# More filler products on TensorE ahead of the first modulation rows

## The chip, the cores and the metric

The kernel runs on one core of a Trainium2 chip. The core has five engines that work side by side, each on its own queue of instructions, in order: TensorE (PE in the profile, matrix products; PEld is its loading of the stationary operand), VectorE (DVE), ScalarE (ACT), GpSimd (POOL) and SyncE (SP), which here issues the transfers. The metric is the device time of one execution in microseconds; lower is better.

## The reference

One layer of a trunk with two parallel groups of heads. 1024 latent tokens and 128 context tokens, each of 1024 channels, are normalised, scaled and shifted by a modulation that comes from a conditioning vector, and multiplied with one input weight; a gated position mixer and a latent attention follow, and an output projection is added to the residual under a gate.

```python
def _front(x, cond, norm_g, w_ada, b_ada, w_in, ...):
    mod = jax.nn.silu(cond) @ w_ada + b_ada
    shift, scale, gate = jnp.split(mod[:, None, :], 3, axis=-1)
    h = _rmsnorm(x, norm_g) * (1 + scale) + shift
    u, v, g_a, c_q, c_kv, k_rope, g_b = _split_in(h @ w_in)
...
def _back(x, gate, a_out, attn, g_b, w_o):
    y = jnp.concatenate([a_out, attn * jax.nn.silu(g_b)], axis=-1) @ w_o
    return x + gate * y
```

All inputs are float32: `w_ada` is 1024 x 3072, `w_in` 1024 x 2496. What matters for the change is the first line: no column of `h` can be made before the shift and scale of its 128 channels are there, and these are a product of the conditioning vector with a slice of `w_ada`.

## The kernel before

The 1152 tokens are nine tiles of 128 (eight latent, one context), the 1024 channels eight slices k of 128. The first stage makes, slice by slice, the modulation, the transposed and modulated tokens `h` (split into a high and a low part, so that three products of them give the accuracy of float32), and the v projection of the tokens, accumulated in PSUM over the slices (`vacc`).

For slice k the stage does the following.

- `load_k(k)` (L376) has SyncE load the slice of `w_ada` in two halves of 512 KB (`load_ada`, L318, one transfer each, L322; each half holds four of the eight blocks of the contraction) and the v weights (`load_wv`, L282).
- `mod_rows(k)` (L330) makes the modulation rows: for each half i four products, one for each strip j of 32 columns of the array, into four strips of the PSUM tile `modp`. Each product of float32 is two instructions in the trace, so a half is eight.
- `mod_copy(k)` (L338): VectorE copies the rows to SBUF (`rows`).
- `mod_cols(k)` (L342): two products with `sel` add the four strips and turn the rows into columns, again in `modp`.
- `mod_act(k)` (L346): ScalarE adds the bias and the norm's gain and writes the columns `at`.
- `h_pe(k, g)` (L432): TensorE transposes three token tiles into `xT`; `h_ev(k, g)` (L436): ScalarE and VectorE modulate them with `at` and split them into the high and low part (`area`).
- `v_block` and `v_block_late` (L439, L443) add the slice to `vacc`.

Ahead of slice 0, token tiles 0 to 2 are loaded, their squares are summed and they are scaled by the root of their mean (ScalarE, VectorE and GpSimd). Behind the first group's modulation the same is done with tiles 3 to 5, in the queues of ScalarE and VectorE.

TensorE, ScalarE, VectorE and GpSimd run this stage in the order in which the lines are written (`manual_schedule`, L455), and so does SyncE; no planner moves anything here. `keep_warm(n)` (L458) writes n products of the identity with a matrix of ones into a PSUM tile `warm` that nothing reads: filler products. They wait for no other engine but for the identity at the start. Before the change there are 24 at the start (L462), and 6, 4, 3 and 2 between the products of slices 0 and 1 (L494 to L506). In TensorE's queue the start is: 24 fillers, `mod_rows(0)`, `mod_cols(0)`, three transposes, 6 fillers, the first products of `vacc`.

Of the kernel before, what the change touches and what calls it, by code (L numbers as in the profile page):

```python
# [81 lines left out]
def f32(ap):  # L82
    return ap.bitcast(F32)
# [3 lines left out]
def tile_hymba_step(ctx: ExitStack, tc: tile.TileContext, I, O):  # L87
# [198 lines left out]
    def load_x(t, i):  # L286
        xt[t] = slot(i, f"x{t}", [1024])
        nc.sync.dma_start(xt[t], I["x"][t])

    def load_x_aside(t):  # L290

        c0 = 2 * P * t - 9 * P
        xt[t] = mixA[:, :, c0 : c0 + 256]
        nc.sync.dma_start(xt[t], I["x"][t].rearrange("p (h c) -> p h c", h=4))
# [6 lines left out]
    def split_w1(k, raw, n, pre):  # L301
        h_ = w1.tile([P, n], F32R, tag=f"wh{k}", name=f"{pre}h{k}")
        l_ = w1.tile([P, n], F32R, tag=f"wl{k}", name=f"{pre}l{k}")
        pool_copy(h_, raw)
        G.tensor_tensor(l_, raw, f32(h_), op=ALU.subtract)
        return h_, l_
# [20 lines left out]

    modp = psa.tile([P, 512], F32, tag="acc", name="modp")

    def mod_rows(k):  # L330


        for i in range(2):
            for j in range(4):
                kk = 4 * i + j
                T.matmul(modp[32 * j : 32 * j + 32, 0:256], csp[:, kk, :], ada[k][kk], start=i == 0, stop=i == 1)

    def mod_copy(k):  # L338
        rowsb[k] = va.tile([P, 256], F32, tag="acc", name=f"rows{k}", bufs=2)
        V.tensor_copy(rowsb[k], modp[:, 0:256])  # L340

    def mod_cols(k):  # L342
        for c in range(2):
            T.matmul(modp[:, 256 + 2 * c : 258 + 2 * c], rowsb[k][:, c * P : (c + 1) * P], sel, start=True, stop=True)

    def mod_act(k):  # L346
        S.activation(at[:, k, :, 0], modp[:, 256:258], AF.Identity, bias=badaT[:, k, 0:1])
        S.activation(at[:, k, :, 1], modp[:, 258:260], AF.Identity, bias=gbias[:, k : k + 1], scale=normg[:, k : k + 1])
# [27 lines left out]
    def load_k(k):  # L376
        if k < NK:
            ada[k] = load_ada(k, ADA[k % 3])
            load_wv(k)
# [7 lines left out]
    def load_w2(i):  # L387
        w2raw[i] = slot(4 + i % 2, f"w2r{i}", [8, P])
        nc.sync.dma_start(w2raw[i], I["w_t"][i])
# [11 lines left out]
    def square(eng, t, out):  # L401
        junk = vb.tile([P, 1024], BF16, tag="junk" if eng is S else "junkV", name=f"junk{t}")
        if len(xt[t].shape) == 3:
            junk = junk.rearrange("p (h c) -> p h c", h=4)
        if eng is S:
            S.activation(junk, xt[t], AF.Square, accum_out=out)
        else:
            V.scalar_tensor_tensor(junk, xt[t], 1.0, xt[t], op0=ALU.mult, op1=ALU.mult, accum_out=out)

    def scale_x(eng, t, r):  # L410
        if eng is S:
            S.activation(xt[t], xt[t], AF.Copy, scale=r)
        elif eng is G:
            G.tensor_scalar(xt[t], xt[t], r, 0.0, op0=ALU.mult, op1=ALU.add)
        else:
            V.tensor_scalar(xt[t], xt[t], r, None, op0=ALU.mult)

    def row_roots(ssq):

        root = vb.tile([P, 3], F32, tag="xroot", name="xroot", bufs=2)  # L420
        v = vb.tile([P, 3], F32, tag="x3v", name="x3v", bufs=2)
        r = vb.tile([P, 3], F32, tag="x3r", name="x3r", bufs=2)
        u = vb.tile([P, 3], F32, tag="x3t", name="x3t", bufs=2)
        S.activation(root, ssq, AF.Sqrt, bias=epsb, scale=1.0 / 1024.0)
        V.tensor_scalar(v, ssq, 1.0 / 1024.0, EPS, op0=ALU.mult, op1=ALU.add)
        V.reciprocal(r, root)
        V.tensor_tensor(u, r, r, op=ALU.mult)
        V.scalar_tensor_tensor(u, u, -0.5, v, op0=ALU.mult, op1=ALU.mult)
        V.scalar_tensor_tensor(r, u, 1.5, r, op0=ALU.add, op1=ALU.mult)
        return r  # L430

    def h_pe(k, g):  # L432
        xps[k, g] = pst.tile([P, 512], F32, tag="t", name=f"xT{k}{g}")
        transposes(k, [3 * g, 3 * g + 1, 3 * g + 2], xps[k, g])

    def h_ev(k, g):  # L436
        modulate(k, g, xps[k, g][:, :GW])

    def v_block(k, ts_):  # L439
        for t in ts_:  # L440
            v_terms(k, t, vacc[t])

    def v_block_late(k, ts_):  # L443

        for t in ts_:
            g, j = t // 3, t % 3
            a = hh[k, g][:, j * P : (j + 1) * P]
            T.matmul(vacc[t], a, wvh[k], start=k == 0, stop=False)
            T.matmul(vacc[t], a, wvl[k], start=False, stop=False)
        for t in ts_:  # L450
            g, j = t // 3, t % 3
            T.matmul(vacc[t], hl[k, g][:, j * P : (j + 1) * P], wvh[k], start=False, stop=False)

    engines = {mybir.EngineType.PE, mybir.EngineType.Activation, mybir.EngineType.DVE, mybir.EngineType.Pool}
    with tc.manual_schedule(engines=engines):  # L455
        warm = psa.tile([P, 512], F32, tag="acc", name="warm")

        def keep_warm(n):  # L458
            for _ in range(n):
                T.matmul(warm[:, 0:P], ident, ones, start=True, stop=True)  # L460

        keep_warm(24)  # L462
        for t in (0, 1, 2):
            load_x(t, 6 + t)
        load_k(0)
        for t in (3, 4, 5):
            load_x(t, 6 + t)
        load_k(1)
        load_k(2)
        for t in range(5):  # L470
            vacc[t] = psa.tile([P, 512], F32, tag="acc", name=f"vacc{t}")
        ssq = [vb.tile([P, 3], F32, tag="ssq", name=f"ssq{i}", bufs=2) for i in range(2)]
        for j, eng in enumerate((S, V, S)):
            square(eng, j, ssq[0][:, j : j + 1])
        r0 = row_roots(ssq[0])
        for j, eng in enumerate((S, V, G)):
            scale_x(eng, j, r0[:, j : j + 1])
        wvh[0] = w1.tile([P, 512], F32R, tag="wh0", name="vh0")
        wvl[0] = w1.tile([P, 512], F32R, tag="wl0", name="vl0")
        S.copy(wvh[0], wvr[0])  # L480
        mod_rows(0)
        mod_copy(0)
        mod_cols(0)
        mod_act(0)
        G.tensor_tensor(wvl[0], wvr[0], f32(wvh[0]), op=ALU.subtract)
        h_pe(0, 0)
        h_ev(0, 0)
        for j, eng in enumerate((S, S, V)):
            square(eng, 3 + j, ssq[1][:, j : j + 1])
        r1 = row_roots(ssq[1])  # L490
        for j, eng in enumerate((S, V, V)):
            scale_x(eng, 3 + j, r1[:, j : j + 1])
        wvh[1], wvl[1] = split_w1(1, wvr[1], 512, "v")
        keep_warm(6)  # L494
        v_block_late(0, (0, 1, 2))
        keep_warm(4)
        mod_rows(1)
        mod_copy(1)
        keep_warm(3)
        h_pe(0, 1)  # L500
        mod_cols(1)
        h_pe(1, 0)
        h_ev(0, 1)
        mod_act(1)
        h_ev(1, 0)
        keep_warm(2)  # L506
        v_block_late(0, (3, 4))
        load_k(3)
        h_pe(1, 1)
        mod_rows(2)  # L510
        h_ev(1, 1)
        mod_copy(2)
        wvh[2], wvl[2] = split_w1(2, wvr[2], 512, "v")
        v_block_late(1, (0, 1))
        for k in range(2, NK):

            more = k + 1 < NK
            load_k(k + 2)
            mod_cols(k)
            h_pe(k, 0)  # L520
            h_pe(k, 1)
            mod_act(k)
            h_ev(k, 0)
            h_ev(k, 1)
            if more:
                wvh[k + 1], wvl[k + 1] = split_w1(k + 1, wvr[k + 1], 512, "v")
                mod_rows(k + 1)
                mod_copy(k + 1)
            v_block(k - 1, (0, 1, 2, 3, 4) if k > 2 else (2, 3, 4))
            if k == 2:  # L530
                for t in (6, 7, 8):
                    load_x_aside(t)
            if k == 4:
                load_w2(0)
                load_w2(1)
                nc.sync.dma_start(wsT, I["wsT"])
                nc.sync.dma_start(bsb, I["b_s"].broadcast_to([P, 512]))
                nc.sync.dma_start(kvg, I["kv_g"].broadcast_to([P, P]))
                ssq2 = vb.tile([P, 3], F32, tag="ssq", name="ssq6", bufs=2)
                for j, eng in enumerate((S, V, V)):  # L540
                    square(eng, 6 + j, ssq2[:, j : j + 1])
            if k == 5:
                r2 = row_roots(ssq2)
                for j, eng in enumerate((G, G, V)):
                    scale_x(eng, 6 + j, r2[:, j : j + 1])
# [217 lines left out]
    for i in range(3, 12):  # L763
# [10 lines left out]
        if i >= 4:  # L774
            k = i - 4
# [832 lines left out]
```

## Time and profile before

| | before |
|---|---|
| median of three runs | 635.0 us (634.12 to 635.34) |
| the profiled execution | 633.38 us |
| its span, first to last instruction | 631.6 us |
| mean granted clock of TensorE | 0.995 |
| TensorE busy | 614.2 us, 97% of the span |
| VectorE busy | 366.5 us, 58% |
| ScalarE busy | 259.4 us, 41% |
| GpSimd busy | 181.8 us, 29% |

The profile shows one execution. Busy is the time that an engine's instructions cover; a matrix product is pipelined, so its row is longer than the distance to the next one, and the pace is read from the starts. "PEclk" is the clock that the throttle granted to TensorE, 1.00 being full. The rest of the text counts time in us from the start of the span.

### The profile page before, as it was taken

The numbers are of one execution on the slowest core, as the hardware profiler recorded it, in microseconds if no ns is written. First come the engines' busy times: TensorE is split into PE (matmuls) and PEld (weight loads), VectorE is DVE, ScalarE is ACT, GpSimd is POOL, SyncE is SP. The second block draws the span as 40 slices with busy tenths as digits, with TensorE's granted clock in tenths as the row PEclk, the third lists the DMA queues.
The fourth block names the chain that finished last, engine by engine and source line by source line (L and its number), as shares of the span: only waits on it lengthen the run. The fifth ranks groups of instructions, "written<-read, shape, count | busy, mean of one in ns | idle before, by whom it ended". The sixth has DMA issues, their size and how long they took to land.

```text
span 631.6 us, 9907 instructions
## 1 busy us (share of the span) xinstructions
PE 614.2 (97%) x3733; PEld 557.1 (88%) x3733; DVE 366.5 (58%) x907; ACT 259.4 (41%) x615; POOL 181.8 (29%) x217
## 2 busy tenths in 40 slices
PE   7999999999999999999979999999999999999995
PEld 6677889999999999999967999999999988888884
DVE  3666447048556200667866665776766755487655
ACT  8456753112111111455646556555555543132212
POOL 2545123247532510433443221332222341000001
PEclk9999999999999999999989999999999999999999
DMA  8993100042322320000010000000101012524311
GB/s 324 353 356 107 34 0 2 1 141 109 113 92 72 110 88 13 25 2 1 2 39 1 2 2 0 1 1 35 34 1 34 33 68 87 181 100 134 104 64 66
DMA packets 17120, 46.32 MB, mean 73 GB/s; under 512 B 1953, under 2 KB 6449, under 8 KB 17073
## 3 DMA queue, kind: packets, MB, share of 16 engines
q1 hardware_dynamic: 16928, 45.51, 21.1%
q8 instruction: 29, 0.48, 0.3%
q10 hardware_dynamic: 144, 0.20, 0.1%
q14 instruction: 19, 0.15, 0.1%
HBM read 40.87 MB, written 4.83 MB: 72 GB/s over the span
## 4 chain that ended last, share of the span: by engine, by line
PE 91%; DVE 4%; ACT 2%; DMA 1%; issue 1%; SPq 0%; ACTq 0%
PE tp L670 6%; PE tp L150 6%; PE tp L152 6%; PE tp L151 6%; PE pT L1134 5%; PE w L1383 5%; PE w L1382 5%; PE w L1381 5%; PE s L1087 3%; PE o L1158 3%; PE o L1160 3%; PE s L1088 3%; PE s L1089 3%; PE s L1090 3%; PE o L1159 3%; PE s L1091 3%
## 5 line engine op out<-in xcount | busy, mean ns | idle before, releaser
L104 DVE TENSOR_TENSOR pl<-pT,ph 128x512 fp32r<-128x512 f32 x81 | 55.5, 687 | 48.0 <-ACT ph L1138 47.8
L1078 POOL TENSOR_SCALAR e<-e,rs 128x1280 f32<-128x1280 f32 x32 | 43.0, 1343 | 134.1 <-DVE rs L1077 116.3
L152 PE MATMUL tp<-area,w2l 128*128 128x384 f32 x216 | 72.5, 336 | 0.0
L150 PE MATMUL tp<-area,w2h 128*128 128x384 f32 x216 | 72.5, 336 | 0.0
L151 PE MATMUL tp<-area,w2h 128*128 128x384 f32 x216 | 72.5, 336 | 0.0
L1072 ACT ACTIVATE e<-s,nb,scl 128x256 f32<-128x256 f32 x64 | 56.1, 881 | 37.6 <-DVE nb L1066 37.6
L1138 ACT CAST ph<-pT 128x512 fp32r<-128x512 f32 x80 | 45.4, 589 | 43.5 <-PE pT L1134 40.6
L1134 PE MATMUL pT<-ident,e 128*128 128x128 f32 x320 | 47.8, 272 | 0.7 <-DVE pl L104 0.7
L1158 PE MATMUL o<-ph,vh 128*128 128x256 f32 x160 | 47.8, 299 | 0.0
L104 DVE TENSOR_TENSOR w2l<-w2r,w2h 128x1024 fp32r<-128x1024 f32 x12 | 20.2, 1685 | 46.1 <-POOL w2h L107 46.1
L1160 PE MATMUL o<-ph,vl 128*128 128x256 f32 x160 | 44.9, 281 | 0.0
L1159 PE MATMUL o<-pl,vh 128*128 128x256 f32 x160 | 44.7, 280 | 0.0
L1383 PE MATMUL w<-area,ml 128*128 128x512 f32 (+1 forms) x114 | 43.2, 379 | 0.0
L1134 PEld LDWEIGHTS pT<-ident,e 128*128 128x128 f32 x320 | 37.5, 140 | 4.4 <-DVE pl L104 1.5
L1062 DVE TENSOR_REDUCE m<-s 128x1 f32<-128x1024 f32 x32 | 38.9, 1216 | 4.0 <-PE s L1091 4.0
L150 PEld LDWEIGHTS tp<-area,w2h 128*128 128x128 f32 x216 | 40.5, 188 | 0.6 <-issue 0.5
L151 PEld LDWEIGHTS tp<-area,w2h 128*128 128x128 f32 x216 | 40.5, 188 | 0.2
L152 PEld LDWEIGHTS tp<-area,w2l 128*128 128x128 f32 x216 | 40.5, 188 | 0.0
L1087 PE MATMUL s<-kch,area 128*128 128x512 f32 (+2 forms) x100 | 39.5, 395 | 0.6 <-DVE area L104 0.6
L670 PE MATMUL tp<-area,w2h 128*128 128x384 f32 x144 | 37.4, 340 | 0.0
L1089 PE MATMUL s<-kch,area 128*128 128x512 f32 (+2 forms) x100 | 35.8, 358 | 0.0
L1088 PE MATMUL s<-kcl,area 128*128 128x512 f32 (+2 forms) x100 | 35.7, 357 | 0.0
(309 smaller groups left out, 1590.0 us busy)
## 6 DMA issues: line engine op xcount, KB each, us to landing
ada<-in_ada_ss SPq DMA_DIRECT2D x16, 512.0 KB, 10.9
w2r<-in_w_t SPq DMA_DIRECT2D x12, 512.0 KB, 4.3
xr<-in_x SPq DMA_DIRECT2D x9, 512.0 KB, 5.1
adag<-in_ada_g SPq DMA_DIRECT2D x8, 512.0 KB
wor<-in_w_o SPq DMA_DIRECT2D x8, 512.0 KB, 3.4
out_y<-y SPq DMA_DIRECT2D x8, 512.0 KB, 2.7
x<-in_x SPq DMA_DIRECT2D x6, 512.0 KB, 8.7
wvr<-in_w_v SPq DMA_DIRECT2D x8, 256.0 KB, 8.6
```

The costliest lines, as they stand in the source:

```text
L104: V.tensor_tensor(lo, src, f32(hi), op=ALU.subtract)
L150: T.matmul(ps, wh, xh, start=j == 0, stop=False)
L151: T.matmul(ps, wh, xl, start=False, stop=False)
L152: T.matmul(ps, wl, xh, start=False, stop=j == n - 1)
L670: T.matmul(tps[i, g][:, :GW], w_[i][:, k, :], x_[k, g], start=k == 0 and j == 0, stop=k == NK - 1 and j == 2)
L1072: S.activation(e[:, sl], src, AF.Exp, bias=nb, scale=scl[:, t : t + 1], accum_out=su[:, i : i + 1])
L1087: T.matmul(ps, qh_, kch[:, sl], start=True, stop=False)
L1134: T.transpose(ps[:, w : w + P], es[t, h][:, c * P : (c + 1) * P], ident)
L1158: T.matmul(o, vh[:, kt, :], ph[:, sl], start=c == 0, stop=False)
L1159: T.matmul(o, vh[:, kt, :], pl[:, sl], start=False, stop=False)
L1160: T.matmul(o, vl[:, kt, :], ph[:, sl], start=False, stop=c == n - 1)
L1383: T.matmul(ps, b, woh[k][:, c0:c1], start=False, stop=k == NK - 1)
```

## The change

Three calls are changed, all in TensorE's queue ahead of the first modulation columns. The fillers at the start are 32 in place of 24. `mod_rows` gets a parameter: with `between=4`, which slice 0 alone uses, four fillers stand between the products of the first and of the second half (`keep_warm(0)` ahead of the first half does nothing). Four more fillers stand between the call that copies the rows, `mod_copy(0)`, and `mod_cols(0)`; the copy is VectorE's, so in TensorE's queue they follow the second half's products. Together 16 fillers are added. No transfer, no copy and no other engine's instruction is added or removed.

```diff
-    def mod_rows(k):
+    def mod_rows(k, between=0):
         for i in range(2):
+            keep_warm(i * between)
             for j in range(4):
                 kk = 4 * i + j
                 T.matmul(modp[32 * j : 32 * j + 32, 0:256], csp[:, kk, :], ada[k][kk], start=i == 0, stop=i == 1)
...
-        keep_warm(24)
+        keep_warm(32)
...
-        mod_rows(0)
+        mod_rows(0, 4)
         mod_copy(0)
+        keep_warm(4)
         mod_cols(0)
         mod_act(0)
```

## The prediction

> **What bounds the kernel now.** I read the page's busy table and its chain first, then the stretch in which the change lies, instruction by instruction.
>
> ```profile
> span 631.6 us, 9907 instructions
> PE 614.2 (97%) x3733; PEld 557.1 (88%) x3733; DVE 366.5 (58%) x907; ACT 259.4 (41%) x615; POOL 181.8 (29%) x217
> ...
> PE 91%; DVE 4%; ACT 2%; DMA 1%; issue 1%; SPq 0%; ACTq 0%
> ```
>
> TensorE is the bound: 97% of the span is covered, and 91% of the chain that ended last is its own work. What matters is therefore not whether TensorE has idle time somewhere, but whether a product added to its queue finds idle time just where it is put. The next view is its timeline over the stretch from the first filler product (L460) to the second layer of modulation rows.
>
> ```profile
> 1.36 7.06 PE L460 MATMUL warm<-ones,ident 128*128 128x128 f32 x48 [1.36 <-POOL ident masks.py:199]
> 9.62 0.64 PE L336 MATMUL modp<-ada,csp 128*32 128x256 f32 x8 [1.20 <-DMA ada<-in_ada_ss]
> 10.80 0.64 PE L336 MATMUL modp<-ada,csp 128*32 128x256 f32 x8 [0.54 <-DMA ada<-in_ada_ss]
> 11.99 0.61 PE L344 MATMUL modp<-sel,rows 128*128 128x2 f32 x4 [0.55 <-DVE rows L340]
> 12.46 0.52 PE L352 MATMUL xT<-ident,x 128*128 128x128 f32 x3
> 12.82 1.50 PE L460 MATMUL warm<-ones,ident 128*128 128x128 f32 x12
> ...
> 16.25 1.05 PE L460 MATMUL warm<-ones,ident 128*128 128x128 f32 x8
> 17.23 1.29 PE L336 MATMUL modp<-ada,csp 128*32 128x256 f32 x16
> 18.45 0.94 PE L460 MATMUL warm<-ones,ident 128*128 128x128 f32 x6
> 19.22 0.49 PE L352 MATMUL xT<-ident,x 128*128 128x128 f32 x3
> ```
>
> Each row is start, length, engine, line, operation and, in brackets, the idle time ahead of it with its cause. The three holes that the change fills stand there: 1.20 us until the first half of the weights has landed, 0.54 us until the second half has, and 0.55 us while VectorE copies the rows. The 24 filler products are 48 instructions, so one call of the loop body is two.
>
> The chain of this stretch in order of time says what comes late now:
>
> ```profile
> 3.06 7.70 DMA ada<-in_ada_ss
> 10.80 0.68 PE modp L336 x8
> 11.51 0.44 DVE rows L340
> 11.99 0.61 PE modp L344 x4
> 12.60 0.39 PE xT L352 x3
> 12.98 1.34 PE warm L460 x12
> ```
>
> The second half of the weights, landed at 10.80, is the last transfer for which the chain waits: 7.70 us of 631.6 is 1.2%, which is the whole DMA share of the page's chain. Behind it the only waits of TensorE are these (us in total, times, longest):
>
> ```profile
> PE kT L959 <- DVE krl L104: 3.8, 1, 3.8
> PE modp L344 <- DVE rows L340: 0.8, 2, 0.5
> PE pT L1134 <- DVE pl L104: 0.7, 2, 0.4
> PE s L1087 <- DVE area L104: 0.6, 1, 0.6
> PE at L1321 <- ACT e L1312: 0.4, 1, 0.4
> PE vacc L452 <- DVE area L104: 0.4, 1, 0.4
> ```
>
> None is for a transfer. All are for VectorE or ScalarE, which work on what TensorE gave them.
>
> **The price of a filler.** The same tile's rows, over the fast stretch and over the slow one ahead of it (count, durations, first and last start):
>
> ```profile
> L460 PE MATMUL warm<-ones,ident x31: 275/275/275, 4.8 to 8.1; 128*128 128x128 f32 x31
> L460 PE MATMUL warm<-ones,ident x13: 421/421/582, 1.4 to 4.1; 128*128 128x128 f32 x13
> ```
>
> The durations overlap, so the price is the pace: 3.3 us over 30 steps is 0.11 us an instruction from about 4.4 us on, and 2.7 over 12 is 0.22 ahead of that. Eight instructions with the handover to the next modulation group are 17.23 - 16.25 = 0.98 us.
>
> One group of eight modulation products, up to a filler behind it, is read from the second group of layer 1, whose weight load stands at 17.88:
>
> ```profile
> 17.88 0.16 PEld L336 LDWEIGHTS modp<-ada,csp 128*32 128x32 f32 x8 [0.49 <-DMA ada<-in_ada_ss]
> ```
>
> 18.45 - 17.88 is 0.57 us.
>
> **The change part by part.** Nothing is removed and no transfer, copy or wait of another engine is added. 16 products, 32 instructions, are added to TensorE's queue in three places, and whatever stands behind them in that queue waits for them.
>
> First, 8 more products ahead of the first half: 16 x 0.11 = 1.8 us. The last filler now starts at 8.1; with 0.2 us of handover (0.98 less seven steps of 0.11) a modulation product could start at 8.3. With the new ones it starts at 10.1. The first 1.20 us lie in the hole; the rest goes past it, 10.1 against 9.62, 0.5 late.
>
> Second, 4 products between the halves: the first group gives way at 10.1 + 0.57 = 10.7, eight instructions and the handover take 0.98, and the second group starts at 11.7. Its weights were there at 10.80, so TensorE now comes 0.9 late to data that lies ready. The hole of 0.54 held only a part.
>
> Third, 4 products during the row copy: they start at 11.7 + 0.57 = 12.25 and take 8 x 0.11 = 0.9 and a handover of 0.1 to 0.2, so the column products start at 13.15 to 13.25. The copy would have let them start at 11.99 + 0.9 = 12.9. They are at L344, 13.2 against 11.99: **1.2 us late**. Where the fillers fit into the holes they cost nothing, because the wait there covers them; 32 x 0.11 = 3.5 us come in and holes of 1.20 + 0.54 + 0.55 = 2.3 us stand against them, which gives the same 1.2.
>
> Does that delay reach the end? The fillers at 12.82, 16.25 and 18.45 are fixed counts, so they don't shrink. ScalarE and VectorE could catch up only if they ran ahead of TensorE here. Their timelines:
>
> ```profile
> 12.63 0.26 ACT L347 ACTIVATE at<-modp,cst 128x2 f32<-128x2 f32 x1 [0.58 <-PE modp L344]
> 12.79 0.34 ACT L348 ACTIVATE at<-modp,gbias,cst 128x2 f32<-128x2 f32 x1
> ...
> 16.44 0.19 ACT L406 ACTIVATION_READ_ACCUMULATOR junk<-x 128x1 f32 x1
> ...
> 17.79 1.42 DVE L416 TENSOR_SCALAR x<-x,x3r 128x1024 f32<-128x1024 f32 x2
> ```
>
> ScalarE takes the modulation columns at 12.63, right behind the column products, and works without a break to 16.63 (squares of the next three token tiles); their roots and VectorE's scaling follow, done at 19.21, and the transposes that need them are at 19.22. So both chains start from the delayed product and end where TensorE stands. Layer 1's rows save what they wait for their second half now, at most 0.1 us of TensorE, but the transposes behind them wait for the scaling anyway. The transfers are issued by SyncE behind POOL's splits and the tiles they reuse; a modulation tile freed 1 us later moves a load by 1 us at most, for a consumer that is itself later. I take the whole 1.2. The bounds: 0.3 us if the second half lands 0.9 us later than here, so that only the third block sticks out (13.2 - 12.9), and 1.6 if handovers and weight loads cost twice what I took, three times 0.13 us more.
>
> **The sum.** The profiled execution took 633.38 us with its span of 631.6, and 1.2 on that is 634.6. The median of the runs shown is 635.0, 1.6 above it; on that base the forecast is **636.2 us**, 0.19% up. About 0.2%, 1.3 us, is what a measurement of this kernel can tell from no change, so the forecast lies just at that bound.
>
> **A gain that the clock could hold.** Fillers can pay only if the holes slow the clock. The granted clock by stretches (busy of PE, PEld, DVE, ACT, POOL, then PEclk, DMA):
>
> ```profile
> 7.81:11.23 3.42, 1.68 (x22) 0.76 (x20) 1.58 (x6) 2.53 (x5) 0.90 (x1) 1.00 1.01 365
> 321.84:325.25 3.41, 0.33 (x1) 0.14 (x1) 3.26 (x14) 0.53 (x2) 1.10 (x3) 1.00 0.07 19
> 325.25:328.67 3.42, 3.38 (x8) 2.71 (x9) 1.02 (x3) 1.65 (x2) 3.25 (x4) 0.50 0.56 163
> ```
>
> A stretch of 3.4 us with 0.33 us of products was followed by one at 0.50; one with 1.68, the holes in question, was not, and the fillers at 12.82 run 12 to 1.3 us, the fast pace. So here the fillers buy nothing. A lost stretch would cost half of 3.42, 1.7 us.
>
> **Rivals.** *The slow pace lasts longer.* The change of pace at 4.4 us came 3 us behind the first filler in this one execution. Each further us at the slow pace puts the fillers' end back by 1 - 0.11/0.22, half a us. Before, that is hidden up to 9.62; with 32 products there is no room left and it all comes on top. With 1 to 3 us more, the delay is 1.7 to 2.7 us, in the middle 637.2 us. Against it: the one trace shows 3 us. The Trainium skill, "TensorE: Matmul & The Clock Gate", section "What's actually happening", says that the window that sets the clock is free-running and doesn't reset with the kernel, so the point of change moves from run to run; one trace can't show that, and by it the time would be spread upwards as this rival has it.
>
> *The weights land later than in the profiled execution, and the fillers are hidden.* With the second half late by 0.9 us only the 0.3 us of the third block are left: 635.3. With both halves late alike, by 0.5 us or more, the first block is hidden, but a group and four fillers, 0.57 + 0.98 = 1.55 us, still don't fit between halves that are 10.80 - 9.62 = 1.18 us apart: 0.4 + 0.3, 635.7. For it: the median is 1.6 us above the profiled time. Against: nothing says that the front is where those 1.6 us lie.
>
> *Faster: the clock falls in the holes, and the fillers prevent it.* The emptiest 3.41 us of the trace, 8.42 to 11.83, hold 1.28 us of products (two groups of 0.64), between 0.33 that lost the clock and 1.68 that kept it. If the second half of the weights lands 0.9 us later, the same stretch holds 0.64 and a little of the second group, and the stretch behind it, full of work, would run at half clock: 1.7 us. The fillers would then give back 1.7 and cost 0.3: 633.6 us. It decides from about 0.9 us of lateness of the second half, and only if some 0.7 us of products are too little to keep the clock, which no row says.
>
> **How the numbers follow.** The forecast has 0.47, of which 0.28 lie over the bound of 1.3 us and 0.19 within; the longer slow pace 0.22, all slower; the hidden fillers 0.16, within; the clock saved 0.15, of which 0.14 faster. Together slower 0.50, same 0.36, faster 0.14. The range goes from 634.4 (hidden fillers at 635.3, less the 0.9 us by which the lowest of the runs, 634.12, lies under the median) to 637.8 (the slow pace 3 us longer); it leaves out most of the saved clock. For the forecast alone it is 635.9 to 636.6.
>
> **What would show it.** In the changed profile: 64 filler instructions up to about 10.2, the first group without a wait for its weights at about 10.1, the second at 11.7, the column products at 13.2, the transposes now at 19.22 at 20.4, and TensorE's wait for VectorE at L959 as long as now. I am wrong if the two groups still wait for their weights (hidden), if the change of pace comes past 5.4 us (rival one), or if a profile of either kernel shows a granted clock of 0.5 near 12 us (rival three).

## The result and the profile after

The changed kernel takes 636.72 us in the median of 22 runs (635.87 to 639.08), the kernel before 634.99 us in 22 (632.8 to 637.46). The ratio is 1.0028 with a 95% interval from 1.0017 to 1.0039: slower by 1.7 us. The profiled execution took 635.87 us with a span of 634.1, 2.5 us more than the span before.

TensorE's timeline of the front after the change (start, length, engine, line, operation; L461, L337 and L345 are L460, L336 and L344 of before):

```profile
1.36 8.86 PE L461 MATMUL warm<-ones,ident 128*128 128x128 f32 x64 [1.36 <-POOL ident masks.py:199]
10.15 0.64 PE L337 MATMUL modp<-ada,csp 128*32 128x256 f32 x8
10.72 1.16 PE L461 MATMUL warm<-ones,ident 128*128 128x128 f32 x8
11.81 0.64 PE L337 MATMUL modp<-ada,csp 128*32 128x256 f32 x8
12.38 1.16 PE L461 MATMUL warm<-ones,ident 128*128 128x128 f32 x8
13.37 0.51 PE L345 MATMUL modp<-sel,rows 128*128 128x2 f32 x4
...
20.66 0.49 PE L353 MATMUL xT<-ident,x 128*128 128x128 f32 x3
```

The three waits are gone, and each product comes within 0.2 us of its forecast: 10.15, 11.81 and 13.37 against 10.1, 11.7 and 13.2. The column products are 1.4 us later than at 11.99 before. The transposes, forecast at 20.4, stand at 20.66. From there on the sum of the prediction does not hold, in three places.

First, the lateness shrinks. VectorE's subtractions (L104) before:

```profile
21.17 1.10 DVE L104 TENSOR_TENSOR area<-hf,area 128x384 fp32r<-128x384 f32 x1
...
24.84 0.88 DVE L104 TENSOR_TENSOR area<-hf,area 128x384 fp32r<-128x384 f32 x1
```

GpSimd's subtraction beside them, before:

```profile
20.57 1.29 POOL L305 TENSOR_TENSOR vl<-wvr,vh 128x512 fp32r<-128x512 f32 x1
```

VectorE's subtractions after the change:

```profile
22.60 0.56 DVE L104 TENSOR_TENSOR area<-hf,area 128x384 fp32r<-128x384 f32 x1
...
25.73 0.56 DVE L104 TENSOR_TENSOR area<-hf,area 128x384 fp32r<-128x384 f32 x1
```

Before, the first one began while GpSimd worked (20.57 to 21.86) and took 1.10 us; 1.4 us later it meets nothing and takes 0.56. With the second, 0.54 + 0.32 = 0.86 us of the delay are given back: the row copy of slice 2 stands at 25.64 before and at 26.20 after, 0.56 late.

Second, VectorE's order is not the same. The low part of the first channel weights (w2l, 1.2 us), traced in the next stage, stands at another place of its queue. VectorE's timeline there, before:

```profile
47.35 0.56 DVE L104 TENSOR_TENSOR area<-hf,area 128x384 fp32r<-128x384 f32 x1
47.82 0.42 DVE L340 COPY rows<-modp 128x256 f32<-128x256 f32 x1
48.16 0.16 DVE L425 TENSOR_SCALAR x3v<-ssq 128x3 f32<-128x3 f32 x1
48.23 0.17 DVE L426 RECIPROCAL x3r<-xroot 128x3 f32<-128x3 f32 x1
48.31 1.20 DVE L104 TENSOR_TENSOR w2l<-w2r,w2h 128x1024 fp32r<-128x1024 f32 x1
```

And after the change:

```profile
47.27 1.21 DVE L104 TENSOR_TENSOR w2l<-w2r,w2h 128x1024 fp32r<-128x1024 f32 x1
48.40 0.67 DVE L360 TENSOR_SCALAR hf<-xT,at 128x384 f32<-128x384 f32 x1
49.10 0.56 DVE L104 TENSOR_TENSOR area<-hf,area 128x384 fp32r<-128x384 f32 x1
49.58 0.42 DVE L341 COPY rows<-modp 128x256 f32<-128x256 f32 x1
```

It is five places earlier, ahead of the copy of the rows of slice 6. What was said above of the order of the lines holds within a stage; at the seam of two stages the order came out otherwise (with 28 fillers at the start w2l stays where it was, with 30 it stands earlier; why is not shown). TensorE now waits 1.2 us for these rows and starts at 50.05 the column products that it started at 48.30 before.

Third, the clock behind the wait for the keys, after the change (busy of PE, PEld, DVE, ACT, POOL, then PEclk): two stretches of 3.4 us at half clock, where the profile before had one.

```profile
325.29:328.71 3.42, 2.15 (x5) 1.57 (x6) 2.73 (x10) 2.06 (x4) 2.72 (x5) 0.50 0.40 99
328.71:332.12 3.41, 3.41 (x11) 2.73 (x11) 0.41 (x1) 0.12 (x1) 1.76 (x2) 0.50 0.21 83
```

The last transpose of the keys is 1.75 us late (324.36 before, 326.11 after); a product behind the lost stretches is 2.5 us late (329.84 and 332.36). So the 2.5 us of this pair of profiles are 1.4 - 0.8 + 1.2 and about 0.7 for the second stretch at half clock. A pair of profiles is one execution each. What is typical had to come from runs.

### The profile page after: what moved, and what is told of

Its sections match the earlier page's. It is cut to its first block, busy times and chain, and to the rows that moved or that the text cites. A ratio compares the mean times of both kernels' runs of the same rounds, so it can differ in the third digit from the quotient of the medians.

```text
span 634.1 us, 9970 instructions
## 1 busy us (share of the span) xinstructions
PE 618.3 (98%) x3765; PEld 561.3 (89%) x3765; DVE 366.9 (58%) x907; ACT 259.3 (41%) x615; POOL 177.3 (28%) x217
## 4 chain that ended last, share of the span: by engine, by line
PE 89%; DVE 5%; DMA 3%; ACT 2%; issue 1%; SPq 0%; ACTq 0%; DVEq 0%
PE tp L672 6%; PE tp L150 6%; PE tp L152 6%; PE tp L151 6%; PE pT L1136 5%; PE w L1383 5%; PE w L1385 5%; PE w L1384 5%; PE s L1089 3%; PE o L1160 3%; PE s L1091 3%; PE s L1092 3%; PE s L1090 3%; PE o L1162 3%; PE s L1093 3%; PE o L1161 3%
## 5 line engine op out<-in xcount | busy, mean ns | idle before, releaser
L104 DVE TENSOR_TENSOR pl<-pT,ph 128x512 fp32r<-128x512 f32 x81 | 55.5, 687 | 48.1 <-ACT ph L1140 48.0
L104 DVE TENSOR_TENSOR w2l<-w2r,w2h 128x1024 fp32r<-128x1024 f32 x12 | 20.3, 1690 | 43.4 <-POOL w2h L107 43.4
L1092 PE MATMUL s<-krh,area 128*128 128x512 f32 (+2 forms) x100 | 35.9, 359 | 0.0
```

What stands on the lines that cost most here:

```text
L104: V.tensor_tensor(lo, src, f32(hi), op=ALU.subtract)
```

## Experiments

All kernels compute the same output; fillers write what nobody reads. Medians are of 12 runs (10 in the last one), the kernel before beside them of 33 to 35 (635.1 to 635.2 us); the verdict is the ratio with its interval. The ratio is not that of the medians, and where the two tell different sizes both are given.

**30 and 28 fillers at the start.** These are to part the moved instruction from the lateness: with 28 w2l stays, with 30 it moves.

```diff
-        keep_warm(24)
+        keep_warm(30)      # the second kernel: 28
```

> Before with 30 fillers at the start in place of 24 and nothing else; this is the smallest count at which w2l, VectorE's low part of the first channel weights (1.2 us), stands ahead of the modulation rows of slice 6 in VectorE's order, as it does after the change. The six more fillers are 12 x 0.11 = 1.3 us and end at about 9.65, where the first half of the weights has just landed. Theory of the prediction (what counts is how late TensorE comes out of the front): 0 to 0.1 us over before. Theory of the moved instruction (the loss is the 1.2 us by which w2l delays the row copy): about 1.2 us over before, with a wait of TensorE for the rows of about 1.2 us near 48 us.

> Before with 28 fillers in place of 24; every engine's order of the rest is that of before. The fillers end at about 9.2 us, inside the wait for the weights. Both theories: within 0.2 us of before. If the fillers have a cost or a use of their own (clock, weight loads) it shows here.

With 30: 635.87 us, ratio 1.0005 (0.9991 to 1.0020). With 28: 634.94, ratio 0.9994 (0.9981 to 1.0007). Against before neither differs. Between the medians of the two, on the same chip, lie 0.9 us, of which the instructions of two fillers can be 0.4. That the moved instruction makes up the rest is not shown. The profile with 30 has a wait for rows of 1.1 us, but at another place. GpSimd and VectorE near 30 us:

```profile
29.90 1.29 POOL L305 TENSOR_TENSOR vl<-wvr,vh 128x512 fp32r<-128x512 f32 x1
29.98 1.62 DVE L104 TENSOR_TENSOR area<-hf,area 128x384 fp32r<-128x384 f32 x1
```

And the column products of TensorE that wait:

```profile
31.99 0.61 PE L344 MATMUL modp<-sel,rows 128*128 128x2 f32 x4 [1.12 <-DVE rows L340]
...
49.54 0.61 PE L344 MATMUL modp<-sel,rows 128*128 128x2 f32 x4 [0.21 <-DVE rows L340]
```

The 1.1 us come from a subtraction of VectorE that ran beside GpSimd's and took 1.62 us. Behind the moved w2l, which stands at 47.47, TensorE waits only 0.2 us. In both profiles the slow pace of the first fillers lasts longer than in that of before, and the column products stand at 12.86 and 12.87, 0.9 us late: the wait for the weights did not hide either count wholly, as the expectations had it, and both end level all the same.

**The whole change with w2l held.**

```diff
-        V.reciprocal(r, root)
+        recips.append(V.reciprocal(r, root))
...
-        step(f"w2{i}", "V", 1.14, lambda: lo_of(w2lo[i], w2raw[i], w2hi[i]), [f"w2h{i}"], 3)
+        step(f"w2{i}", "V", 1.14, lambda: lo_of(w2lo[i], w2raw[i], w2hi[i]) if i else lo_after(), [f"w2h{i}"], 3)
+
+    def lo_after():
+        ins = V.tensor_tensor(w2lo[0], w2raw[0], f32(w2hi[0]), op=ALU.subtract)
+        no_sync = mybir.DependencyInfo(mybir.DependencyClass.NoSync, mybir.DependencyReason.DATA)
+        tc.add_manual_dep(ins.ins, recips[2].ins.name, no_sync, reason="order")
```

> All 16 added fillers in their three places, but VectorE's w2l held behind the reciprocal of the third root, where it stands before the change. Theory of the prediction: 1.2 us over before, as the changed kernel without its clock part. Theory of the moved instruction: TensorE leaves the front 1.3 us late, gets 0.8 us of it back by 27 us, because VectorE's subtractions then fall less on GpSimd's, and ends 0.4 to 0.7 us over before.

637.05 us, ratio 1.0027 (1.0012 to 1.0043): as slow as the changed kernel. The theory of the moved instruction falls.

**The changed kernel again**, for a second profile:

> The changed kernel once more, beside the next one on the same chip. All theories: 1.2 to 2.5 us over before, and no execution with the clock lost near 12 us, since its holes are filled.

637.14 us, ratio 1.0026 (1.0009 to 1.0042). In the front its profile is that of the held form almost to the tenth, and unlike the first one. TensorE's first row in the repeat:

```profile
1.36 10.15 PE L461 MATMUL warm<-ones,ident 128*128 128x128 f32 x64 [1.36 <-DVE onesr L231]
```

VectorE's scalings of the next tokens, two instructions:

```profile
20.79 2.33 DVE L417 TENSOR_SCALAR x<-x,x3r 128x1024 f32<-128x1024 f32 x2
```

GpSimd's subtraction beside them:

```profile
20.64 1.27 POOL L305 TENSOR_TENSOR vl<-wvr,vh 128x512 fp32r<-128x512 f32 x1
```

And the clock there, with the columns of the stretches above:

```profile
20.77:24.19 3.42, 2.61 (x19) 1.85 (x16) 2.66 (x3) 1.80 (x3) 2.07 (x3) 1.00 0.97 382
24.19:27.60 3.41, 3.41 (x13) 2.92 (x12) 2.43 (x4) 1.14 (x4) 2.11 (x3) 0.50 0.98 363
```

The same 64 instructions take 10.15 us in place of 8.86: the slow pace lasted 1.3/0.5 = 2.6 us longer, since a us at the slow pace costs half a us. The column products come out 2.7 us late, the scalings now start beside GpSimd's subtraction and take 2.33 in place of 1.42 us, the transposes wait for them, and behind that the clock is lost for one stretch. Of the 2.61 us of products in the stretch ahead of the loss 1.20 are transposes, the first three of which wait for scalings. The same stretch, `xT` alone:

```profile
20.77:24.19 3.42, 1.20 (x5) 0.74 (x6) 0.00 (x0) 0.65 (x1) 1.00 0.97 382
```

**One part at a time, w2l held**: the first part (32 at the start), and the second and third (4 between, 4 during the copy).

```diff
-        keep_warm(24)
+        keep_warm(32)      # first kernel alone
...
-        mod_rows(0)
-        mod_copy(0)
+        mod_rows(0, 4)     # second kernel alone
+        mod_copy(0); keep_warm(4)
```

> The first part alone, 32 fillers at the start, with w2l held where it stands before the change. The column products come out of the front 0.5 to 2 us late, by how long the slow pace lasts (to 4.4 us in the profile of before, to 7.5 us in that of the run with 28 fillers). Theory that the lateness reaches the end: 0.5 to 1.5 us over before. Rival (a floor near 50 us, where the weights of slice 7 land: TensorE waited 1.0 and 1.3 us for them in the runs with 28 fillers and with the fillers ahead of the keys, so that up to about 1 us of lateness is taken up there): 0 to 0.4 us.

> The second and third part alone, 24 fillers at the start, 4 between the halves and 4 during the row copy, with w2l held where it stands before the change. The slow pace is hidden up to 9.6 us, so the column products are 0.4 + 0.3 = 0.7 us late whenever it ends. Theory that the lateness reaches the end: 0.7 us over before. Rival (floor near 50 us): 0 to 0.2 us, and the two parts together with the first cost more than their sum, because only the sum goes past the floor.

The first part: 635.04 us, ratio 0.9990 (0.9975 to 1.0005). The second and third: 634.43, ratio 0.9981 (0.9965 to 0.9996). Neither ends over before; the latter even gains 1.2 us by the ratio, 0.7 by the medians, and both together cost 1.7 to 1.8. As forecasts of the time, both forms of the theory that lateness simply adds up have failed. Whether it is not passed on, or is passed on and made up by a higher clock, the times alone do not tell; see the clock over all executions below.

**Half the start.** 28 at the start, 4 and 4, w2l held:

> 28 fillers at the start, 4 between the halves, 4 during the row copy, w2l held where it stands before the change: four fillers fewer than the held form of the whole change, and four more than the second and third part alone. The column products are 0.7 to 1.9 us late, by how long the slow pace lasts. Theory that the cost is lateness beyond about 1.4 us (VectorE's scalings then meet GpSimd's subtraction of slice 1, 1.7 in place of 0.75 us in the held form): most executions stay under it, within 0.6 us of before. Theory that each added filler behind 2.3 us costs its 0.22 us: 0.9 us under the held form, so about 1 us over before.

635.35 us, ratio 0.9997 (0.9983 to 1.0010). Four products fewer than in the held form take away the whole cost, 1.7 us (1.8 against the changed kernel on the same chip), where their own time is 0.9. In its profile the slow pace lasts longer too, 56 instructions in 9.10 us where the first profile has 64 in 8.86, and yet the column products stand at 13.61 only. That is 1.6 us late, past the 1.4 us from which the first theory expected a cost. TensorE's timeline:

```profile
1.35 9.10 PE L460 MATMUL warm<-ones,ident 128*128 128x128 f32 x56 [1.35 <-DVE onesr L231]
...
13.61 0.51 PE L344 MATMUL modp<-sel,rows 128*128 128x2 f32 x4
```

The scalings overlap GpSimd's work by less:

```profile
19.30 1.79 DVE L416 TENSOR_SCALAR x<-x,x3r 128x1024 f32<-128x1024 f32 x2
```

In four profiles lateness, by the start of the column products, and the two scalings go together: 11.99 us before and 1.42, 13.37 and 1.42 (the change, first profile), 13.61 and 1.79, 14.65 and 2.33 (the change, second profile). Lateness is not what decides, though. In the profile of the second and third part alone the weights landed late, at 10.44, and a stretch of clock was lost. TensorE, GpSimd and VectorE there:

```profile
15.21 0.51 PE L344 MATMUL modp<-sel,rows 128*128 128x2 f32 x4
...
20.05 1.27 POOL L305 TENSOR_TENSOR vl<-wvr,vh 128x512 fp32r<-128x512 f32 x1
...
21.77 1.42 DVE L416 TENSOR_SCALAR x<-x,x3r 128x1024 f32<-128x1024 f32 x2
```

The column products are 3.2 us late, the latest of all, and the scalings take 1.42 us, because GpSimd is done at 21.32, before they start. What counts is whether the scalings fall into GpSimd's work.

**Fillers ahead of the last key transpose**, in two forms of their target, with 24 at the start as before.

```diff
-            (0.25, lambda: q_rope_T(8)),
+            (0.25, lambda: q_rope_T(8)), (0.0, lambda: [T.matmul(spare[0], ident, ones, start=True, stop=True) for _ in range(16)]),
             (0.15, lambda: keys(8, 1, 0)),
```

`spare[0]` is `ps[:, GW:]` of the last `q_nope` in the first form, `ps[:, 256:384]` of the last `q_rope` in the second.

> Before with its own 24 fillers at the start and 16 fillers at another place: ahead of the last transpose of the keys (L959), where TensorE waits 3.8 us for VectorE and the granted clock drops to 0.5 for 3.4 us behind it. 16 fillers are 32 x 0.11 = 3.6 us and fit into the wait. Theory that fillers pay only where a stretch of 3.4 us is nearly empty: the drop near 325 us goes and 1.7 us are gained. Rival (the fillers come between TensorE and the keys, or the drop comes from something else than idle time): 0 to 0.5 us over before.

> 16 fillers in the wait ahead of the last key transpose again, but into columns of a product that has long been read, so that they don't wait for ScalarE's reading of their tile (0.35 us in the first form) and end ahead of the keys. The clock does not drop near 325 us. Theory (fillers pay only where a stretch of 3.4 us is nearly empty): 1.5 to 2 us under before, 0.2 more than the first form. Rival (that gain was spread between executions): within 0.5 us of before.

633.80 us, ratio 0.9975 (0.9957 to 0.9992), and 634.18, ratio 0.9971 (0.9955 to 0.9986): faster by 1.6 and 1.8 us by the ratio, 1.4 and 0.9 by the medians. Neither profile has the drop near 325 us. The target made no difference that shows. The profile of the second form, whose front is that of before, shows what the profile of before did not. TensorE's timeline, then the clock by stretches:

```profile
1.36 7.36 PE L460 MATMUL warm<-ones,ident 128*128 128x128 f32 x48 [1.36 <-POOL ident masks.py:199]
9.65 0.64 PE L336 MATMUL modp<-ada,csp 128*32 128x256 f32 x8 [0.93 <-ACT xroot L424]
10.84 0.64 PE L336 MATMUL modp<-ada,csp 128*32 128x256 f32 x8 [0.55 <-DMA ada<-in_ada_ss]
```

```profile
8.45:11.86 3.41, 1.55 (x19) 0.43 (x17) 1.90 (x7) 2.55 (x5) 1.33 (x1) 1.00 1.00 386
11.86:15.28 3.42, 3.25 (x15) 3.26 (x16) 0.24 (x2) 2.14 (x6) 1.53 (x2) 0.50 1.02 417
15.28:18.69 3.41, 3.41 (x11) 2.85 (x11) 2.60 (x9) 2.51 (x6) 0.07 (x1) 0.50 1.04 406
```

The weights land when they did before, yet the holes lose the clock, for two stretches: the stretch that decides began at 8.45 in place of 7.81, and holds 1.55 in place of 1.68 us of products. Behind it TensorE is 3 us later than in the profile of before, at the first slice's last products.

**12 fillers at the start.**

```diff
-        keep_warm(24)
+        keep_warm(12)
```

> 12 fillers at the start in place of 24. They end between 5.6 and 6.5 us, and TensorE is empty for 3 to 4 us until the weights land. Theory that the fillers at the start do work for the clock: the first slices run at half pace for one or two stretches of 3.4 us, 1 to 3 us over before. Rival (the fillers are idle work here): 0, or a little faster.

636.53 us, ratio 1.0012 (0.9999 to 1.0024): 1.4 us over before by the medians, but not clearly slower by the ratio, though its profile loses the clock for three stretches in a row. The stretch that loses it and the first one lost:

```profile
5.40:8.81 3.41, 0.82 (x7) 0.62 (x6) 1.31 (x3) 3.17 (x5) 0.00 (x0) 1.00 0.96 299
8.81:12.22 3.41, 2.16 (x16) 0.43 (x16) 1.58 (x6) 2.36 (x5) 1.59 (x1) 0.50 1.01 400
```

**Both gains together**: the fillers ahead of the keys (second form) with 28 at the start, and with 24, 4 and 4.

> 28 fillers at the start and 16 ahead of the last key transpose. The front has no stretch of 3.4 us empty enough to lose the clock (none of 12 executions with 28 had it, against 13 of 35 of before), and the wait near 322 us is filled too. Theory that both gains add: 1.5 to 2.5 us under before, with no execution over 635.5 us. Rival (the floor near 50 us or the spread swallows one): 1 us under before, as the fillers ahead of the keys alone.

> 24 fillers at the start, 4 between the halves, 4 during the row copy, w2l held, and 16 fillers ahead of the last key transpose. The first hole of 1.2 us is left as it is before. Theory that a late landing of the weights still loses the clock there in some executions (one profile of the second and third part alone shows it, with 1.4 us of products in the stretch): 1 to 2 us under before, with some executions as slow as before. Rival (the second and third holes alone decide): as the form with 28, 1.5 to 2.5 us under before.

633.32 us, ratio 0.9972 (0.9958 to 0.9986), and 632.56, ratio 0.9958 (0.9943 to 0.9973). The second is faster than before by 2.7 us, the most of all kernels here. Against the expectation it has no execution as slow as the median of before: its ten runs lie between 632.0 and 634.29. With 28 it is 1.8 us, inside the 1.5 to 2.5 expected of both gains, and no execution lies over 633.99; but the fillers ahead of the keys alone gave 1.6 and 1.8, so that the gains add up is not shown there. TensorE's timeline of the better one, ahead of the keys:

```profile
322.83 3.74 PE L1040 MATMUL qr<-ones,ident 128*128 128x128 f32 x32
326.40 0.27 PE L963 MATMUL kT<-ident,kvn 128*128 128x128 f32 x1
326.63 0.50 PE L1091 MATMUL s<-kch,area 128*128 128x512 f32 x1
```

And its clock there, which stays at full speed:

```profile
324.00:328.00 4.00, 4.00 (x31) 3.60 (x30) 2.99 (x12) 1.25 (x4) 2.58 (x4) 1.00 0.30 77
```

**The clock over all executions.** Each execution has its mean granted clock. At 0.988 or less were 13 of 35, 11 of 35 and 10 of 33 executions of before, in the three groups of runs. None was in 12 each with 28 and 30 at the start, with either set of parts alone, and with 28, 4 and 4; in the changed kernel it was 2 of 22 and 3 of 12, in its held form 3 of 12. With 12 at the start it was 9 of 12. The count misses single stretches: one profile of the second and third part alone loses the clock from 11.22 to 14.63 and has 0.990. And it counts more than the front: with the fillers ahead of the keys, and the front of before, it was none of 24.

Where the drop near 325 us is gone the front stands alone. There 0.994 or less was found in 7 and 9 of 12 executions with the front of before, in 1 of 12 with 28 at the start, and in none of 10 with 24, 4 and 4. By this count the front of before loses the clock in more than half of the executions (16 of 24), and both ways of filling it prevent that (1 of 22).

Kernels can also be compared at one mean clock. At 0.991 the executions of before have medians of 634.75, 634.70 and 634.55 us (12, 11 and 8 of them); 635.25 with 28 at the start (6), 635.62 with the first part alone (7), 635.50 with the second and third (4), 635.82 with 28, 4 and 4 (3); 636.68 and 637.14 for the changed kernel (11 and 5), 636.58 for its held form (5). So the parts are not free: at an equal clock they lie about 0.5 to 1.3 us over before, and end level with it while they have no executions at the lowest clocks. The whole change lies 1.8 to 2.6 us over. These are few executions each, and the mean also takes in the end of the span, where TensorE has nothing left to do (0.50 from 629.04 to 631.60 in the profile of before): an indication, no proof.

## Why the prediction was right, and where its working failed

*The holes and the price of a filler.* Right: 32 instructions at 0.11 us against holes of 2.3 us, 1.4 us late for 1.2. The 0.2 lie in the handovers, inside the bound of 1.6.

*"Does that delay reach the end? ... I take the whole 1.2."* This step is not borne out, and that the sum came out near, 1.3 us against 1.7, is in part luck. In the first pair of profiles 0.8 of it was given back by 27 us, which I had ruled out by saying that the chains of ScalarE and VectorE end where TensorE stands; I had not looked at how long their instructions take beside GpSimd. Either set of parts alone ends level with before or under it, with column products 1.0 us late in the profile of the first (12.95). The cost of 1.7 us appears between 28 and 32 fillers at the start. At an equal mean clock the parts do cost something, so a part of the lateness may well arrive and be made up by the clock, a gain that the forecast put at nothing.

*"No transfer, copy or wait of another engine is added"*, and a queue order that stays. Wrong in the profile: w2l moved, and a wait of 1.2 us came with it (0.2 in the repeat). It isn't what the change costs: held back, the kernel is as slow.

*The longer slow pace.* Given 0.22, and with 2.7 us as its upper end. The second profile and the held form show just this, 2.7 us late with a slow pace to about 7 us (4.4 + 2.6), past the 5.4 that the prediction gave as the sign of this rival. So in two of three profiles the rival that I put behind the forecast is what happened. What I had missed is its further price: the scalings meet GpSimd, and a stretch of clock goes. One execution of each run has a profile, so how many of the others are of this kind is not known.

*"So here the fillers buy nothing."* Right for the profile of before, wrong for the kernel: where the drop near 325 us is gone, more than half of the executions with the same front have a mean clock that shows a lost stretch, and a profile shows that loss at 1.55 us of products in the stretch, without later weights. The rival gave it the right place and price (1.7 us a stretch) and the wrong condition. The change lowers the count of executions at 0.988 or less from a third to 5 of 34, and so its 1.7 us look like a difference of a larger cost, about 2 us at an equal clock, and a gain; the second and third part alone show a gain, 1.2 us by the ratio and 0.7 by the medians.

*The hidden fillers.* All three profiles of the change and its held form have no wait for the weights of slice 0: the rival is refuted there. That 28 at the start cost nothing does not speak for it either, since in their profile the first group started at 10.71 without a wait.

*Open.* Why the cost appears between 28 and 32 is not shown. How it is shared between the later start, the collision with GpSimd and the clock behind it was not parted, and neither was what a wait for the weights of slice 7 takes up (TensorE waited 0.5 and 1.3 us in the profiles with 28 and with the first fillers ahead of the keys, where the expectation of the first part has 1.0 for the former, which is the wait of the weight load; none in those of the held form and of the repeat). Why the stretch from 20.77, with 2.61 us of products by the rows, loses the clock when 1.68 kept it elsewhere, is open too. Without its transposes 1.41 us are left, under the 1.55 that lost it elsewhere, so it would fit if transposes did not count; no run tests that.

## What to carry to other kernels

Fillers pay by the stretch, not by the hole: ask how full the emptiest 3.4 us are, and put fillers where data can't come earlier, with room behind them for a slow pace that ends 3 us later than in the one profile at hand. Filling the wait ahead of the keys, behind which the profile of before has 3.4 us at half clock, gained more (1.6 and 1.8 us by the ratio) than any filling of the front alone (1.2), though the intervals overlap. A delay on the bounding engine is not passed on as a constant: look at what the delayed instructions of VectorE will meet on GpSimd, and compare the order of every queue after a change, also those that it does not touch.

## What the runs showed of the hardware

The point at which the pace changes moves between executions: 64 fillers took 8.86 us in one and 10.15 in another, 48 took 7.06, 7.36 and 8.00. It is read from the pace of the rows: the granted clock of the profile is 1.00 in the slow part too (0.99 to 4.40 before). The Trainium skill, "TensorE: Matmul & The Clock Gate", section "What's actually happening", says that the window is free-running; these rows agree.

The Trainium skill, "TensorE: Matmul & The Clock Gate", section "HAM oscillation — how this bites in real kernels", gives as its rule that no gap of TensorE be longer than about 3.4 us. In the front of the second profile with fillers ahead of the keys the longest hole was 0.93 us, and the clock was lost: in these rows it goes by the fill of a whole stretch, 0.33, 0.82, 1.39 (from 7.80, second and third part alone) and 1.55 us of 3.41 losing it and 1.68 keeping it. The stretch with 2.61 us, 1.20 of them transposes, is the exception. Getting it back takes more: stretches at half clock with 2.15 us of products (325.29 after the change) and with 3.25 (11.86 in the second profile with fillers ahead of the keys) were each followed by another one, those with 3.38 (325.25 before) and 3.41 were not.

VectorE's pair of scalings of 128x1024 takes 1.42 us, and 2.33 when it starts behind GpSimd's subtraction; its 128x384 subtraction takes 0.56, and 1.10 or 1.62 beside it. The Trainium skill, "SBUF — State Buffer", section "Who interferes with whom", says of instructions of the two engines that need the ports they share that the one that starts first holds them for its whole instruction and the other one is blocked. The rows agree in kind: GpSimd's instruction ended at 21.91, and the pair of scalings that began at 20.79 lost 0.9 us.
